# Gate and up of a two-layer decoder step: eight block products become seven on 14 of 22 tiles

## The chip, the cores and the metric

One of the NeuronCores of a Trainium2 chip runs the whole program in one launch. The metric is the device time of that program in microseconds (us); lower is better. Engines are named as in the profile: PE is TensorE (matmul) and PEld its weight load, DVE is VectorE, ACT is ScalarE, POOL is GpSimd, SP is the engine whose queue issues most transfers.

## The reference

One inference step of a two-layer decoder over 512 prompt tokens and 8 x 4 sample tokens, model width 1024, in fp32. Each layer is a macaron block:

```
x += 1/2 * SwiGLU(RMSNorm(x))                    # ffn1, width 2816
x += W_out [ tokmix(RMSNorm(x)) ; memxattn(...) ]
x += 1/2 * SwiGLU(RMSNorm(x))                    # ffn2, width 2816

def swiglu_half(x, g, w_gu, w_down):
    h = rmsnorm(x, g)
    gate, up = jnp.split(h @ w_gu, 2, axis=-1)
    return 0.5 * ((jax.nn.silu(gate) * up) @ w_down)
```

Layer 0 mixes tokens by gated linear attention, layer 1 by sliding-window attention with sinks over one shared key and value projection; both also attend to 256 memory tokens. A final RMSNorm follows. The caches, states and memory projections are outputs too. The four feed forwards hold most of the multiplications.

## The kernel before, in words

The residual stream stays in SBUF, transposed: eight tiles of 128 features for each of two token halves. Half 0 has 288 columns (256 prompt tokens and the 32 sample tokens), half 1 has 256. `NH` holds these widths, `KD` is 8.

Every fp32 product is made from three matmuls of the faster fp32r type: `split_into` (lines 291 to 299) has ACT copy a tile to its rounded high part, and DVE subtracts to get the low part; line 320 then runs high x high, high x low and low x high. `dense` (lines 310 to 323) does this for one weight tile of up to 128 outputs: for each half in its list it runs all eight contraction tiles, three matmuls each, into one PSUM bank. All its matmuls are recorded on line 321. `weight` (301 to 308) loads the raw tile through SP's queue into one of three tiles `wr`, and splits it into `wh` and `wl` (`WB` has their counts).

A feed forward (`ffn`, lines 405 to 439) has 22 tiles f of 128 gate and 128 up outputs, cut into three chunks by `CHUNKS`. For every f it runs gate, then up, applies the activation (ACT) and the multiplication (DVE), and splits the product; after a chunk's f's it runs the eight down tiles m and adds them to the residual. One f's gate, one f's up, or one m is a unit: the generator yields after each. Chunks 1 and 2 run over both halves, each weight serving both. Chunk 0 (9 f's) runs for each half by itself, so that its units can fill the waits of the other half's attention: `layer` (1090 to 1140) weaves attention steps with such units, by the counts in `FILL` (lead, pad, hold, last, more). After chunk 2's gathering the sums of squares, `rstd` (355 to 383) makes the reciprocal root mean square through small matmuls, and `normed` (393 to 402) scales the eight tiles and splits them: the inputs of what follows.

Within an engine, instructions run in the order that the tile framework's planner writes from its own estimate of the timeline; `high_priority(offset=...)` lets an instruction be placed as if it stood so many instructions earlier. `AHEAD` (6000) is used for splits of weights and reads of banks, `SOON` (6500) for a norm, `LEAD` for attention. Temporaries are `NU` slots of 288 columns, handed out in the order in which they were given back. Tiles tagged `v`, `ld` and `ml` serve attention: values, states and masks, and memory caches.

Of the kernel before, what the change touches and what calls it, by code (L numbers as in the profile page):

```python
# [32 lines left out]
FT = FF // P  # L33
CHUNKS = ((0, 9), (9, 15), (15, 22))
EARLY = 2 * CHUNKS[0][1] + KD
# [144 lines left out]
class Ring:  # L180
    """A few tiles that temporaries take in turn."""

# [22 lines left out]
class Banks:  # L205
    """PSUM banks that a stream takes in turn."""

# [23 lines left out]
class Build:  # L231
    NU, NV, NLD, NML = 102, 13, 8, 3
    WB = (3, 3, 3)
    MIX = 10
    FIRST, AHEAD, SOON, LEAD = 20000, 6000, 6500, 3000
    FILL = ((7, 1, 8, 2, 3), (8, 2, 6, 0, 6))

    def __init__(self, ctx, tc, d):
        self.tc, self.nc, self.d = tc, tc.nc, d
        self.cp = ctx.enter_context(tc.tile_pool(name="cp", bufs=1))  # L240
        self.wp = ctx.enter_context(tc.tile_pool(name="wp", bufs=2))
        self.up = ctx.enter_context(tc.tile_pool(name="up", bufs=1))
        self.pp = ctx.enter_context(tc.tile_pool(name="pp", bufs=1, space=PSUM))
        self.acc, self.seen = [[], [], []], [0, 0, 0]
        self.free = deque(range(self.NU))
        self.used, self.early = {}, {}
        banks = [self.pp.tile([P, 512], F32, tag=f"bank{i}", name=f"bank{i}") for i in range(8)]
        self.bd, self.bt, self.bm_ = Banks(banks[:3] + banks[5:]), Banks(banks[3:5]), Banks(banks[6:])
        self.sqs, self.xns, self.gas = Ring(self, 3), Ring(self, 2), Ring(self, 4)

# [33 lines left out]

# [1 line left out]
    def split(self, src, n):  # L286
# [14 lines left out]
    def weight(self, src, kc, m, name):  # L301
        nc = self.nc
        r = self.wp.tile([P, kc, m], F32, tag="wr", name=name + "r", bufs=self.WB[0])
        nc.sync.dma_start(r, src)
        h, l = (self.wp.tile([P, kc, m], F32R, tag="w" + e, name=name + e, bufs=b) for e, b in zip("hl", self.WB[1:]))
        with self.tc.high_priority(offset=self.AHEAD):
            self.split_into(h, l, r)
        return h, l

    def dense(self, src, parts, name, m=P, order=None):  # L310
# [18 lines left out]

# [1 line left out]
    def stats(self, x, h):  # L331
# [23 lines left out]
    def rstd(self, h, banks=None, keep=True):  # L355
        """1 / rms of every token, the same on all partitions, from the sums of squares over the blocks."""
        acc, self.acc[h], self.seen[h] = self.acc[h], [], 0
# [45 lines left out]

# [1 line left out]
    def ffn(self, tag, c, halves, xs, gathered=(), tanh=False):  # L405
# [3 lines left out]
        gs = {h: [] for h in halves}  # L409
        parts = [xs[h] for h in halves]  # L410
        for f in range(f0, f1):
# [28 lines left out]

# [1 line left out]
    def mem_load(self, k):  # L442
# [45 lines left out]

# [1 line left out]
    def mem_prompt(self, l, mq, mo):  # L490
# [115 lines left out]

# [1 line left out]
    def blocks(self, h):  # L608
# [254 lines left out]

# [1 line left out]
    def rope(self, ps, out, h, n=P):  # L865
# [51 lines left out]

# [1 line left out]
    def in_b(self, h, xs, s):  # L919
# [168 lines left out]

# [1 line left out]
    def layer(self, l, project, attend, w_out, xs):  # L1090
        """xs: the halves' inputs of the first feed forward; returns the inputs of what follows."""
        s = [Share(), Share()]
# [3 lines left out]
        def enter(h, norm):  # L1096
# [4 lines left out]
            return out  # L1101

        lead, pad, hold, last, more = self.FILL[l]
        drain(self.ffn(f1, 1, (0, 1), xs), self.ffn(f1, 2, (0, 1), xs, gathered=(0,)))
        self.drop(xs[0])
        late = self.ffn(f1, 0, (1,), xs, gathered=(1,), tanh=True)
# [24 lines left out]
        drain(self.out_proj(w_out, s[1].toks + s[1].mo, 1))  # L1131
        out[1] = enter(1, f"ffn2_{l}")
        drain(early)
        drain(self.ffn(f2, 1, (0, 1), out), self.ffn(f2, 2, (0, 1), out, gathered=(0,)))
        self.drop(out[0])

# [31 lines left out]
    def run(self):  # L1168
# [8 lines left out]
        self.vt, self.state, self.st = [None] * 5, [None] * GH, [None] * NB  # L1177
        self.x = [[], []]
        with self.tc.high_priority(offset=self.FIRST):
            self.gains = self.const("gains")  # L1180
# [26 lines left out]
        r = self.rstd(1)  # L1207
        xs[1] = self.normed(1, "ffn1_0", r)
        self.drop(r)
# [28 lines left out]
        drain(self.shared_kv(1, xk))  # L1238
        xs[1] = self.normed(1, "ffn1_1", r)
        self.drop(r)  # L1240
# [78 lines left out]
```

## Time and profile before

| | us |
|---|---|
| median of 3 runs | 2229.39 (2227.86 to 2230.09) |
| profiled execution, span from first to last instruction | 2228.3 |
| PE busy | 2192.8 (98%) |
| DVE busy | 1242.6 (56%) |
| ACT busy | 922.9 (41%) |
| mean granted TensorE clock | 0.990 |

The profiled execution's own time is its span and little around it: the span lies 1.1 us under the median of the runs. The profile lists the busy time of each engine, groups of instructions by line and tile, the waits and what ended them, and a timeline. A matmul's row gives its duration from start to the last result, about 0.28 to 0.30 us, while the next one starts after 0.12 to 0.13 us: the price of a matmul in a stream is the distance of starts, that is, a stretch of time over the number in it.

### The profile page before, as it was taken

How to read it: one execution, taken by the hardware profiler on the slowest of the kernel's cores; microseconds unless marked ns; L12 is line 12 of the kernel's file. 1: busy time of each engine (PE TensorE's matmuls, PEld its weight loads, DVE VectorE, ACT ScalarE, POOL GpSimd, SP SyncE). 2: the span in 40 equal slices, each digit the busy share in tenths (PEclk: the TensorE clock that was granted, in tenths of full speed). 3: DMA queues.
4: the chain of work that ended last, by engine and by line, in shares of the span. 5: the costliest groups of instructions: out<-in, count | busy, mean ns of one | idle time of the engine just before them, and what ended most of it. 6: DMA issues, size and time to landing. Idle time of an engine off the chain costs nothing.

```text
span 2228.3 us, 40781 instructions
## 1 busy us (share of the span) xinstructions
PE 2192.8 (98%) x16822; PEld 2106.3 (95%) x16822; DVE 1242.6 (56%) x2556; ACT 922.9 (41%) x1767; POOL 35.2 (2%) x69
## 2 busy tenths in 40 slices
PE   7999999999999999999999999999999999999998
PEld 6999999998699999999999999999888889999998
DVE  7633336586568865333577433337767766433355
ACT  4522224664556554222455322224534544322244
POOL 5000000000000000000000000000000000000000
PEclk8999999999999999999999999999989999999999
DMA  8532223444455344232364522224434334322244
GB/s 268 169 112 84 95 86 124 142 129 136 136 167 168 111 143 127 76 101 86 110 199 160 172 92 90 86 86 148 139 113 134 124 100 150 101 81 95 85 153 135
DMA packets 91546, 279.30 MB, mean 125 GB/s; under 512 B 11440, under 2 KB 25280, under 8 KB 91328
## 3 DMA queue, kind: packets, MB, share of 16 engines
q1 hardware_dynamic: 90784, 276.17, 39.4%
q8 instruction: 132, 2.16, 0.4%
q10 hardware_dynamic: 576, 0.52, 0.1%
q14 instruction: 54, 0.44, 0.1%
HBM read 270.33 MB, written 7.70 MB: 125 GB/s over the span
## 4 chain that ended last, share of the span: by engine, by line
PE 96%; ACT 1%; DVE 1%; issue 1%; DMA 1%; POOL 0%; SPq 0%; DVEq 0%; ACTq 0%
PE bank L321 85%; PE bank L960 1%; PE bank L735 1%; PE bank L575 1%; PE bank L502 1%; PE bank L855 1%; PE bank L974 1%; PE bank L523 1%; PE bank L973 1%; PE bank L847 1%; PE bank L549 0%; PE bank L365 0%; PE bank L377 0%; PE bank L514 0%; PE bank L995 0%
## 5 line engine op out<-in xcount | busy, mean ns | idle before, releaser
L294 ACT ACTIVATE u<-u 128x288 fp32r<-128x288 f32 (+2 forms) x308 | 124.3, 417 | 164.3 <-DVE u L425 130.6
L433 DVE SCALAR_TENSOR_TENSOR x<-bank,x 128x288 f32<-128x288 f32 (+1 forms) x192 | 84.6, 440 | 183.1 <-PE bank L321 182.8
L425 DVE TENSOR_TENSOR u<-u,bank 128x288 f32<-128x288 f32 (+1 forms) x176 | 76.7, 436 | 145.6 <-PE bank L321 144.4
L295 DVE TENSOR_TENSOR u<-u,u 128x288 fp32r<-128x288 f32 (+2 forms) x308 | 128.3, 430 | 33.5 <-ACT u L294 31.9
L420 ACT ACTIVATE u<-bank 128x288 f32<-128x288 f32 (+1 forms) x122 | 47.5, 390 | 98.7 <-PE bank L321 98.6
L321 PE MATMUL bank<-u,d0h 128*128 128x288 f32 (+1 forms) x352 | 70.3, 290 | 0.0
L321 PE MATMUL bank<-u,d1h 128*128 128x288 f32 (+1 forms) x352 | 68.9, 289 | 0.0
L321 PE MATMUL bank<-u,d2h 128*128 128x288 f32 (+1 forms) x352 | 68.3, 290 | 0.2 <-DVE x L598 0.2
L321 PE MATMUL bank<-u,d7h 128*128 128x288 f32 (+1 forms) x352 | 68.4, 291 | 0.0
L321 PE MATMUL bank<-u,d3h 128*128 128x288 f32 (+1 forms) x352 | 68.2, 290 | 0.0
L321 PE MATMUL bank<-u,d5h 128*128 128x288 f32 (+1 forms) x352 | 67.9, 290 | 0.1
L321 PE MATMUL bank<-u,d4h 128*128 128x288 f32 (+1 forms) x352 | 67.7, 289 | 0.0
L321 PE MATMUL bank<-u,d6h 128*128 128x288 f32 (+1 forms) x352 | 67.3, 288 | 0.0
L341 ACT ACTIVATE u<-x 128x288 f32<-128x288 f32 (+1 forms) x78 | 32.7, 422 | 64.9 <-DVE x L433 61.7
L321 PEld LDWEIGHTS bank<-u,d0h 128*128 128x128 f32 x352 | 56.2, 188 | 0.9 <-issue 0.8
L321 PEld LDWEIGHTS bank<-u,d7h 128*128 128x128 f32 x352 | 56.0, 190 | 0.8 <-issue 0.8
L321 PEld LDWEIGHTS bank<-u,d5h 128*128 128x128 f32 x352 | 55.3, 189 | 1.2 <-issue 1.2
L321 PEld LDWEIGHTS bank<-u,d4h 128*128 128x128 f32 x352 | 55.4, 188 | 0.7 <-issue 0.6
L321 PEld LDWEIGHTS bank<-u,d1h 128*128 128x128 f32 x352 | 55.7, 188 | 0.4 <-issue 0.4
L321 PEld LDWEIGHTS bank<-u,d2h 128*128 128x128 f32 x352 | 55.5, 189 | 0.3 <-issue 0.2
L321 PEld LDWEIGHTS bank<-u,d3h 128*128 128x128 f32 x352 | 55.6, 189 | 0.2 <-issue 0.2
L399 DVE SCALAR_TENSOR_TENSOR u<-x,gains,u 128x288 f32<-128x288 f32 (+1 forms) x112 | 53.2, 502 | 4.2 <-ACT u L382 4.0
(758 smaller groups left out, 7401.2 us busy)
## 6 DMA issues: line engine op xcount, KB each, us to landing
d0r<-dn_ffn SPq DMA_DIRECT2D x8, 576.0 KB, 3.9
d1r<-dn_ffn SPq DMA_DIRECT2D x8, 576.0 KB, 3.6
d2r<-dn_ffn SPq DMA_DIRECT2D x8, 576.0 KB, 3.9
d3r<-dn_ffn SPq DMA_DIRECT2D x8, 576.0 KB, 3.6
d4r<-dn_ffn SPq DMA_DIRECT2D x8, 576.0 KB, 3.8
d5r<-dn_ffn SPq DMA_DIRECT2D x8, 576.0 KB, 3.9
d6r<-dn_ffn SPq DMA_DIRECT2D x8, 576.0 KB, 3.7
d7r<-dn_ffn SPq DMA_DIRECT2D x8, 576.0 KB, 4.3
```

Source lines behind the costliest of these rows:

```text
L294: nc.scalar.activation(h, src, AF.Copy)
L295: nc.vector.tensor_tensor(out=l, in0=src, in1=h.bitcast(F32), op=ALU.subtract)
L321: self.nc.tensor.matmul(ps, w[:, k, :], x, start=i == 0 and j == 0, stop=i == kc - 1 and j == 2)
L341: nc.scalar.activation(sq, x, AF.Square)
L399: nc.vector.scalar_tensor_tensor(out=t, in0=self.x[h][k], scalar=self.gains[:, g, k:k + 1], in1=r, op0=ALU.mult, op1=ALU.mult)
L420: nc.scalar.activation(a, p, AF.Silu)
L425: nc.vector.tensor_tensor(out=a, in0=a, in1=p, op=ALU.mult)
L433: nc.vector.scalar_tensor_tensor(out=x, in0=po[i], scalar=0.25 if tanh else 0.5, in1=x, op0=ALU.mult, op1=ALU.add)
L502: nc.tensor.matmul(ps[:, b, :], mq[b][rows, tok], kt[b][rows], start=True, stop=True)
L523: nc.tensor.matmul(po[rows, (h // 2) * P:][:, :P], v[mt][:, 64 * h:64 * h + 64], pt[h][:, mt, :], start=mt == 0, stop=mt == 1)
L575: nc.tensor.matmul(po[:, :MT], pt[:, 4 * mt:4 * mt + 4].rearrange("p a t -> p (a t)"), vc[:, mt, :], start=b == 0 and mt == 0, stop=b == N ...
L735: nc.tensor.matmul(pv[:, c * half:(c + 1) * half], lhs[:, c * P:(c + 1) * P], second(rhs[:, c * P:(c + 1) * P]), start=True, stop=True)
```

## The change

The product of the two token halves with gate and up is a 2 x 2 block product: rows are the two halves of the contraction (four tiles each, `HK`), one factor's columns are gate and up, the other's are two token groups. Such a product takes eight block products as written, and seven by the scheme of Strassen and Winograd, at the price of sums of blocks ahead of and behind the products. The change does so for chunks 1 and 2 of every feed forward; `CHUNKS` now gives them 14 of 22 f's, and chunk 0 has 8.

- The token groups are two of 272 columns (`PW`): the first 272 of half 0, and half 1 with the last 16 columns of half 0.
- `pair` makes half 1's inputs (with the 16 columns added), splits them, and makes four forms, that is, sums and differences of input blocks, of four tiles each, also split. `form_tile` puts them in the tiles of attention that stand unused (`HOMES`) and in slots. `enter_pair` calls it after the output projection of half 1 ahead of ffn2; ahead of ffn1 it takes the place of `normed` for half 1.
- `quads` loads an f's gate and up tile together, makes four sums and differences of their halves on DVE, and splits gate, the two tiles of sums, and the second half of up.
- `ffn_pair` runs the seven products of an f, each four contraction tiles by three matmuls of 272 columns. One bank (`pb`) is seeded by ACT with a copy of the first product and then accumulated on. ACT and DVE read partial sums between products. The down tiles run over the two groups of 272, and three instead of two additions bring them to the residual.
- The slots are 97 instead of 102, raw weights keep 3 tiles, high and low parts get 4 each, sums of weights 2; the ring of activations has 6 instead of 4. `FILL` changes its counts.

```
-CHUNKS = ((0, 9), (9, 15), (15, 22))
+CHUNKS = ((0, 8), (8, 15), (15, 22))
+PW = (2 * P + NS + 2 * P) // 2
+HK = KD // 2
...
-    NU, NV, NLD, NML = 102, 13, 8, 3
-    WB = (3, 3, 3)
+    NU, NV, NLD, NML = 97, 13, 8, 3
+    WB = (3, 4, 4, 2)
     MIX = 10
     FIRST, AHEAD, SOON, LEAD = 20000, 6000, 6500, 3000
-    FILL = ((7, 1, 8, 2, 3), (8, 2, 6, 0, 6))
+    FILL = ((6, 1, 7, 2, 6), (7, 2, 5, 0, 9))
+    HOMES = ((13, 8, 3), (8, 8, 3))
 
     def __init__(self, ctx, tc, d):
         self.tc, self.nc, self.d = tc, tc.nc, d
...
         self.used, self.early = {}, {}
         banks = [self.pp.tile([P, 512], F32, tag=f"bank{i}", name=f"bank{i}") for i in range(8)]
         self.bd, self.bt, self.bm_ = Banks(banks[:3] + banks[5:]), Banks(banks[3:5]), Banks(banks[6:])
-        self.sqs, self.xns, self.gas = Ring(self, 3), Ring(self, 2), Ring(self, 4)
+        self.pb, self.pac = Banks(banks[3:5]), Banks(banks[5:])
+        self.sqs, self.xns, self.gas = Ring(self, 3), Ring(self, 2), Ring(self, 6)
 
...
-        h, l = (self.wp.tile([P, kc, m], F32R, tag="w" + e, name=name + e, bufs=b) for e, b in zip("hl", self.WB[1:]))
         with self.tc.high_priority(offset=self.AHEAD):
-            self.split_into(h, l, r)
+            return self.halved(r, name)
+    def halved(self, src, name):
+        h, l = (self.wp.tile(list(src.shape), F32R, tag="w" + e, name=name + e, bufs=b)
+                for e, b in zip("hl", self.WB[1:]))
+        self.split_into(h, l, src)
         return h, l
+    def quads(self, gu, f):
+        nc = self.nc
+        g, u = (self.wp.tile([P, KD, P], F32, tag="wr", name=f"{e}{f}r", bufs=self.WB[0]) for e in "gu")
+        nc.sync.dma_start(g, gu[f])
+        nc.sync.dma_start(u, gu[FT + f])
+        with self.tc.high_priority(offset=self.AHEAD):
+            gh, gl = self.halved(g, f"g{f}")
+            s, t = (self.wp.tile([P, KD, P], F32, tag="ws", name=f"{e}{f}s", bufs=self.WB[3]) for e in "st")
+            nc.vector.tensor_tensor(out=s[:, :HK], in0=u[:, :HK], in1=u[:, HK:], op=ALU.add)
+            nc.vector.tensor_tensor(out=s[:, HK:], in0=s[:, :HK], in1=g[:, :HK], op=ALU.subtract)
+            sh, sl = self.halved(s, f"s{f}")
+            nc.vector.tensor_tensor(out=t[:, :HK], in0=g[:, :HK], in1=u[:, :HK], op=ALU.subtract)
+            nc.vector.tensor_tensor(out=t[:, HK:], in0=g[:, HK:], in1=s[:, HK:], op=ALU.subtract)
+            th, tl = self.halved(t, f"t{f}")
+            uh, ul = self.halved(u[:, HK:], f"u{f}")
+        lo = lambda *w: tuple(a[:, :HK] for a in w)
+        hi = lambda *w: tuple(a[:, HK:] for a in w)
+        return lo(gh, gl), hi(gh, gl), lo(sh, sl), hi(sh, sl), lo(th, tl), hi(th, tl), (uh, ul)
+    def product(self, ps, w, xs, start):
+        wh, wl = w
+        for k, (xh, xl) in enumerate(xs):
+            for j, (a, x) in enumerate(((wh, xh), (wh, xl), (wl, xh))):
+                self.nc.tensor.matmul(ps, a[:, k, :], x, start=start and k == 0 and j == 0,
+                                      stop=k == len(xs) - 1 and j == 2, skip_group_check=True)
 
...
+    def pair(self, norm, r, xa):
+        nc = self.nc
+        g = NORMS.index(norm)
+        ts, cs = [self.u(PW) for _ in range(KD)], [self.u(PW) for _ in range(HK)]
+        xb = [None] * KD
+        forms, self.formed, self.extra = [], 0, []
+        for k in (0, 4, 1, 5, 2, 6, 3, 7):
+            nc.vector.scalar_tensor_tensor(out=ts[k][:, :NH[1]], in0=self.x[1][k], scalar=self.gains[:, g, k:k + 1],
+                                           in1=r, op0=ALU.mult, op1=ALU.mult)
+            nc.vector.tensor_tensor(out=ts[k][:, NH[1]:], in0=xa[k][0][:, PW:].bitcast(F32),
+                                    in1=xa[k][1][:, PW:].bitcast(F32), op=ALU.add)
+        part = lambda k, e: xa[k][e][:, :PW].bitcast(F32)
+        def form(srcs):
+            out = []
+            for s in srcs:
+                h, l = self.form_tile(), self.form_tile()
+                self.split_into(h, l, s)
+                out.append((h, l))
+            forms.append(out)
+        for k in range(HK):
+            nc.vector.tensor_tensor(out=cs[k], in0=ts[k], in1=part(k, 0), op=ALU.subtract)
+            nc.vector.tensor_tensor(out=cs[k], in0=cs[k], in1=part(k, 1), op=ALU.subtract)
+        form(cs)
+        for k in range(HK):
+            nc.vector.tensor_tensor(out=cs[k], in0=ts[k + HK], in1=cs[k], op=ALU.subtract)
+        form(cs)
+        for k in range(HK):
+            xb[k] = self.split(ts[k], PW)
+            nc.vector.tensor_tensor(out=ts[k], in0=ts[k + HK], in1=ts[k], op=ALU.subtract)
+        form(ts[:HK])
+        for k in range(HK):
+            xb[k + HK] = self.split(ts[k + HK], PW)
+            nc.vector.tensor_tensor(out=cs[k], in0=part(k + HK, 0), in1=cs[k], op=ALU.subtract)
+            nc.vector.tensor_tensor(out=cs[k], in0=cs[k], in1=part(k + HK, 1), op=ALU.add)
+        form(cs)
+        self.drop(ts, cs)
+        return xb, forms
+    def form_tile(self):
+        n, self.formed = self.formed, self.formed + 1
+        at = self.HOMES[self.layer_]
+        if n < at[0]:
+            return self.up.tile([P, PW], F32R, tag="v", name="fv", bufs=self.NV)
+        if n < at[0] + at[1]:
+            return self.up.tile([P, PW], F32R, tag="ld", name="fl", bufs=self.NLD)
+        if n < sum(at):
+            return self.up.tile([P, PW], F32R, tag="ml", name="fm", bufs=self.NML)
+        t = self.u(PW, F32R)
+        self.extra.append(t)
+        return t
+    def ffn_pair(self, tag, c, xs, gathered=()):
+        nc = self.nc
+        gu, dn = self.d["gu_" + tag], self.d["dn_" + tag]
+        f0, f1 = CHUNKS[c]
+        xa = [(h[:, :PW], l[:, :PW]) for h, l in xs[0]]
+        xb, (t1, t2, t3, t4) = xs[1], xs["forms"]
+        ga, gb = [], []
+        for bank in self.pb.banks:
+            nc.tensor.matmul(bank[:, :PW], xa[0][0][:, :P], xa[0][0], start=True, stop=True, skip_group_check=True)
+        for f in range(f0, f1):
+            w1, w2, s1, s2, s3, s4, w4 = self.quads(gu, f)
+            pa, pc, pb = (b()[:, :PW] for b in (self.pac, self.pac, self.pb))
+            c5, c2, act = (self.gas.u(PW) for _ in range(3))
+            ahead = lambda: self.tc.high_priority(offset=self.AHEAD)
+            self.product(pa, w1, xa[:HK], True)
+            with ahead():
+                nc.scalar.activation(pb, pa, AF.Copy)
+            self.product(pc, s1, t1, True)
+            self.product(pb, s2, t2, False)
+            with ahead():
+                nc.scalar.activation(c5, pc, AF.Copy)
+            self.product(pa, w2, xa[HK:], False)
+            with ahead():
+                nc.scalar.activation(c2, pb, AF.Copy)
+            self.product(pb, s3, t3, False)
+            with ahead():
+                nc.scalar.activation(act, pa, AF.Silu)
+                nc.vector.tensor_tensor(out=c5, in0=c5, in1=pb, op=ALU.add)
+            self.product(pc, s4, xb[HK:], False)
+            self.product(pb, w4, t4, False)
+            with ahead():
+                nc.vector.tensor_tensor(out=c2, in0=c2, in1=pc, op=ALU.add)
+                nc.scalar.activation(c2, c2, AF.Silu)
+                nc.vector.tensor_tensor(out=act, in0=act, in1=pb, op=ALU.mult)
+                ga.append(self.split(act, PW))
+                nc.vector.tensor_tensor(out=c2, in0=c2, in1=c5, op=ALU.mult)
+                gb.append(self.split(c2, PW))
+            yield
+        for m in range(KD):
+            po = self.dense(dn[m, :, f0:f1, :], [ga, gb], f"d{m}")
+            x0, x1 = self.x[0][m], self.x[1][m]
+            with self.tc.high_priority(offset=self.AHEAD):
+                for x, p in ((x0[:, :PW], po[0]), (x0[:, PW:], po[1][:, NH[1]:]), (x1, po[1][:, :NH[1]])):
+                    nc.vector.scalar_tensor_tensor(out=x, in0=p, scalar=0.5, in1=x, op0=ALU.mult, op1=ALU.add)
+            for h in gathered:
+                self.stats((x0, x1)[h], h)
+            if m == KD - 1:
+                self.drop(ga, gb)
+            yield
...
-        parts = [xs[h] for h in halves]
+        parts = [[(a[:, :NH[h]], b[:, :NH[h]]) for a, b in xs[h]] for h in halves]
...
+        def enter_pair(norm, xs):
+            with self.tc.high_priority(offset=self.SOON):
+                r = self.rstd(1)
+                xs[1], xs["forms"] = self.pair(norm, r, xs[0])
+            self.drop(r)
+        def both(tag, xs):
+            drain(self.ffn_pair(tag, 1, xs), self.ffn_pair(tag, 2, xs, gathered=(0,)))
+            self.drop(xs[0], self.extra)
         lead, pad, hold, last, more = self.FILL[l]
-        drain(self.ffn(f1, 1, (0, 1), xs), self.ffn(f1, 2, (0, 1), xs, gathered=(0,)))
-        self.drop(xs[0])
+        both(f1, xs)
         late = self.ffn(f1, 0, (1,), xs, gathered=(1,), tanh=True)
         mix[0] = enter(0, f"mix_{l}")
         drain(take(late, lead))
...
         drain(take(early, last))
         self.drop(s[1].q if l else [])
         drain(self.out_proj(w_out, s[1].toks + s[1].mo, 1))
-        out[1] = enter(1, f"ffn2_{l}")
+        enter_pair(f"ffn2_{l}", out)
         drain(early)
-        drain(self.ffn(f2, 1, (0, 1), out), self.ffn(f2, 2, (0, 1), out, gathered=(0,)))
-        self.drop(out[0])
+        both(f2, out)
 
...
+        self.layer_ = 0
...
-        xs[1] = self.normed(1, "ffn1_0", r)
+        xs[1], xs["forms"] = self.pair("ffn1_0", r, xs[0])
...
-        xs[1] = self.normed(1, "ffn1_1", r)
+        self.layer_ = 1
+        xs[1], xs["forms"] = self.pair("ffn1_1", r, xs[0])
```

Docstrings and comments that go are left out.

## The prediction

> **What bounds the kernel now.** I read the page's shares and its chain of waits first, then the windows by stage, then the groups by form, then the timeline where the change cuts in.
>
> ```profile
> span 2228.3 us, 40781 instructions
> ...
> PE 2192.8 (98%) x16822; PEld 2106.3 (95%) x16822; DVE 1242.6 (56%) x2556; ACT 922.9 (41%) x1767; POOL 35.2 (2%) x69
> ...
> PE 96%; ACT 1%; DVE 1%; issue 1%; DMA 1%; POOL 0%; SPq 0%; DVEq 0%; ACTq 0%
> ```
>
> TensorE is the bound: it has 35.5 us without work, and 96% of the chain is its own. Fewer matmuls shorten the run, unless another engine becomes the pace. So I need the price of a matmul and the room on DVE and ACT. Windows of line 321 alone (columns: stretch, length, PE busy and count, weight loads, clock, DMA):
>
> ```profile
> 100.00:120.00 20.00, 20.00 (x153) 20.00 (x152) 1.00 0.53 162
> 2160.00:2180.00 20.00, 19.91 (x167) 19.92 (x168) 1.00 0.74 233
> 124.00:172.00 48.00, 48.00 (x384) 48.00 (x383) 1.00 0.29 96
> ```
>
> The first stretch has only half 0 (288 columns): without the two at its edges 151 matmuls, 132 ns each. The second has only half 1 (256 columns): 119 to 120 ns; I take 119. The third is gate and up over both halves: 125 ns, so an f of 96 matmuls takes 12.0 us. The other engines in such a stretch, and in the attention of half 1 in layer 0 (PE, PEld, DVE, ACT, POOL):
>
> ```profile
> 144.00:192.00 48.00, 48.00 (x387) 48.00 (x386) 16.21 (x24) 14.00 (x24) 0.00 (x0) 1.00 0.27 79
> 686.00:818.00 132.00, 131.55 (x1021) 128.29 (x1021) 105.76 (x282) 81.12 (x191) 1.11 (x6) 1.00 0.42 136
> ```
>
> DVE has 4.05 us of work in 12.0 us per f: that is the room the change spends.
>
> **The change, part by part.** *Matmuls.* 13 ns for 32 columns puts 272 at 125.5 ns. Before, a feed forward has 22 x 96 = 2112 gate and up matmuls, half of each width: 1056 x 132 + 1056 x 119 = 265.1 us. After, 8 f's stay (384 x 132 + 384 x 119 = 96.4) and 14 take 7 x 4 x 3 = 84 matmuls of 272 (1176 x 125.5 = 147.6), together 244.0. The down products keep their number and mean width. Saved: 21.1 per feed forward, 84.3 us for four. 272 columns are in no row: at the price of 288 the gain, down products included, would be 36.6 us, at that of 256 it would be 132.6. I take the middle, since the width is the middle. Two dummy matmuls in each of the eight pair stages cost 16 x 0.125 = 2 us. [...]
>
> *DVE and ACT in a paired f.* Groups by form (columns: busy us, mean ns of one, idle before it; five of DVE, of which the fifth, from the windows of 192 to 234 us, splits a down weight, then three of ACT):
>
> ```profile
> L295 DVE TENSOR_TENSOR u<-u,u 128x288 fp32r<-128x288 f32 x150 | 66.7, 454 | 29.0 <-ACT u L294 28.2
> L295 DVE TENSOR_TENSOR u<-u,u 128x256 fp32r<-128x256 f32 x150 | 61.4, 418 | 3.2 <-ACT u L294 2.6
> L295 DVE TENSOR_TENSOR g4l<-g4r,g4h 128x1024 fp32r<-128x1024 f32 x8 | 9.8, 1224 | 1.8 <-ACT g4h L294 1.8
> L399 DVE SCALAR_TENSOR_TENSOR u<-x,gains,u 128x256 f32<-128x256 f32 x56 | 25.5, 479 | 3.2 <-ACT u L382 3.0
> L295 DVE TENSOR_TENSOR d1l<-d1r,d1h 128x768 fp32r<-128x768 f32 x1 | 1.0, 959 | 4.7 <-ACT d1h L294 4.7
> L294 ACT ACTIVATE g4h<-g4r 128x1024 fp32r<-128x1024 f32 x8 | 8.5, 1061 | 8.9 <-PE bank L321 6.7 <-issue 1.6 <-ACT u L987 0.6
> L420 ACT ACTIVATE u<-bank 128x256 f32<-128x256 f32 x52 | 19.1, 367 | 0.0
> L420 ACT ACTIVATE u<-bank 128x288 f32<-128x288 f32 x70 | 28.5, 408 | 98.7 <-PE bank L321 98.6
> ```
>
> On DVE, 512 columns lie midway between 256 and 768: 688 ns; 272 are 436. A paired f has three low parts of 1024 (3.67), four sums and one low part of 512 (3.44) and six operations of 272 (2.62): 9.73 us. ACT has three copies of 1024, one of 512 (about 0.63) and seven of 272 (0.39 to 0.42): 6.6 us. TensorE takes 84 x 125.5 = 10.54 us. In the timeline a low part and what follows it:
>
> ```profile
> 151.12 0.42 DVE L425 TENSOR_TENSOR u<-u,bank 128x256 f32<-128x256 f32 x1 [1.41 <-PE bank L321]
> 152.15 1.23 DVE L295 TENSOR_TENSOR g12l<-g12r,g12h 128x1024 fp32r<-128x1024 f32 x1 [0.60 <-ACT g12h L294]
> 153.29 0.42 DVE L295 TENSOR_TENSOR u<-u,u 128x256 fp32r<-128x256 f32 x1
> 163.12 0.42 DVE L425 TENSOR_TENSOR u<-u,bank 128x256 f32<-128x256 f32 x1 [1.41 <-PE bank L321]
> ```
>
> The next starts 0.09 us before the long one ends, so 14 operations back to back occupy 8.5 us. But each low part waits 0.60 us for its copy where nothing fills in. With 8.5 to 9.7 of 10.54 us, TensorE still paces the f, narrowly; the time would be gone if waits add 2 us.
>
> *Handovers.* Three reads of a bank now stand between products: the copy that seeds the second bank, the copy taken from it, and DVE's sum. Each has one product, 12 x 125.5 = 1.51 us, as cover.
>
> ```profile
> 153.96 0.30 PE L321 MATMUL bank<-u,g11l 128*128 128x288 f32 x1
> 154.35 0.41 ACT L420 ACTIVATE u<-bank 128x288 f32<-128x288 f32 x1 [1.94 <-PE bank L321]
> ...
> 49.08 0.41 ACT L420 ACTIVATE u<-bank 128x288 f32<-128x288 f32 x1
> 49.54 0.53 PE L321 MATMUL bank<-u,u1h 128*128 128x288 f32 x2 [0.29 <-ACT u L420]
> ```
>
> From the last matmul's start to the read 0.39 us, the read 0.39, to the next matmul 0.05: 0.83, of which 0.13 is the matmul's own slot. That leaves 0.8 us. A free engine loses nothing; one that has just begun a 1024 copy (1.06) or low part (1.22) is late by 0.26 or 0.4 us. Bounds per f: 0 to 0.9 us. The big copies come free when a product ends, behind the read that has the same moment and an earlier place, so I take 0.15: 56 x 0.15 = 8.4 us.
>
> *Weight transfers.* Bytes are the same; the ring of three raw tiles now gives up two per f.
>
> ```profile
> u1r<-gu_ffn SPq DMA_DIRECT2D x8, 512.0 KB, 3.7
> ```
>
> The up tile is asked for when the gate's low part of the f before is made, about 1 us before that f starts, and is needed some 6 us later: nothing. If the tile came free an f later, each f would wait up to 3.7 us. The forms also sit in the tiles of the mask, state and memory loads, so those leave SP's queue, and POOL's cast of the masks runs, only after the paired stage:
>
> ```profile
> L743 DVE COPY_PREDICATED u<-masks,bank x40: 266/294/450, 458.2 to 770.1; 128x128 f32<-128x128 uint8 x40
> L844 SPq DMA_DIRECT2D st<-state x16: 312/370/507, 41.1 to 579.2; - x16
> ```
>
> The masks' first reader starts at 458 us and the paired f's of layer 0's first feed forward end near 316 (from 124, 13 f's of 12.0 us and 288 down products of 125 ns): nothing. A load that the queue held ahead of weights would stop TensorE for as long as it waits.
>
> *Pair inputs.* pair() replaces half 1's eight scalings and eight splits (8 x 0.90 = 7.2 us of DVE) by eight scalings (3.8), eight adds of 16 columns (about 1.4 in all, taken as 0.17 each an estimate: 1.1 ns a column as between the rows of 256 and 288, and the same start-up), 24 sums and 24 low parts of 272 (21.0): 26 us, or 20.4 in steps 0.09 shorter. At the entry of ffn1 18 and 14 units of half 0 follow, a unit being 24 x 132 = 3.17 us: 57 and 44 us, which hide it. At ffn2 it starts only after the output projection and the norm:
>
> ```profile
> 846.36 0.40 PE L321 MATMUL bank<-u,op7h 128*128 128x256 f32 x2
> ...
> 858.42 0.88 DVE L399 SCALAR_TENSOR_TENSOR u<-x,gains,u 128x256 f32<-128x256 f32 x2 [0.60 <-ACT u L382]
> ...
> 1879.32 0.28 PE L321 MATMUL bank<-u,op7l 128*128 128x256 f32 x1
> ...
> 1891.14 0.88 DVE L399 SCALAR_TENSOR_TENSOR u<-x,gains,u 128x256 f32<-128x256 f32 x2 [0.36 <-ACT u L382]
> ```
>
> That is 11.8 us after the projection. FILL keeps 6 units there in layer 0 (3 before) and 9 in layer 1 (6 before): TensorE has 19.0 and 28.5 us. The first form is ready at about 20 us, when product 2 wants it at 20.5. The last is ready at 11.8 + 20.4 = 32, wanted by product 7 at 28 and 37.6. The weights' low parts and first reads of the same stretch, about 7.6 us of DVE, come between. Layer 0: 4 to 12 us, I take 10, since both queue on one engine; layer 1: 0 to 6, I take 2. What waits behind is the next f's weights.
>
> *Less fill.* The attention of half 1 gets 16 and 15 units in place of 21 and 20: 5 x 3.17 = 15.8 us less cover each. In layer 0's window above DVE works 105.8 of 132 us, and 116 would be left, so it still fits: 0 to 15.8 each, I take 3 together. The attention of half 0 keeps its number of units.
>
> **Sum:** 2228.3 - 84.3 + 2.0 + 8.4 + 12 + 3 = 2169.4. The median shown, 2229.39, is 1.1 above the profiled span, so 2170.
>
> **Rivals.** *DVE paces the f, mildly.* If 1.5 us of waits per f stay unfilled: 9.73 + 1.5 = 11.2 us, 0.7 above TensorE, 39 us in place of 8.4: 2201. For it: an f leaves DVE under 2 us; against: four f's of rows show DVE idle two thirds, and the split order can be moved.
> *DVE paces it past the old f (slower).* An f has six copy and low-part pairs; if none of their waits (0.55 each) is filled, 9.73 + 3.3 = 13.0 us, 2.5 above TensorE, 140 us: about 2300. It decides at 11.8 us per f, 2 us of unfilled waits. Against: DVE's queue has other ready work in every wait.
> *All hidden.* Handovers free, entries covered: 2228.3 - 82.3 = 2146, with the offset 2148.
> *The entry stall halves the clock.* Clock windows:
>
> ```profile
> 567.60:574.40 6.80, 6.54 (x20) 4.00 (x20) 4.41 (x18) 2.60 (x8) 0.00 (x0) 0.50 0.77 229
> 676.00:684.00 8.00, 5.54 (x48) 5.47 (x49) 5.18 (x10) 6.14 (x11) 0.31 (x1) 1.00 0.53 175
> ```
>
> A gap of 2.4 us left the clock at 1.00; a stretch of 20 matmuls in 6.8 us ran at 0.50. If the entry's stall comes in one piece, 6.8 us at half speed cost 3.4 at each ffn2: 2177. [...] Against it: the stall is spread over four products.
> *It doesn't cut time per matmul:* the bound at 288's price above, 2170 + 48 = 2218.
>
> **How the numbers follow.** Forecast 0.46 (its own range 2155 to 2187), all hidden 0.14, half clock 0.06, DVE mildly 0.18, no cheaper matmul 0.04, DVE past the old f 0.12. 2148 to 2222 leaves out the last and a part of the edges. Within 0.2% (4.5 us, what a measurement can tell) lies only a strip around 11.8 us per f: 0.03. Faster 0.85, slower 0.12.
>
> **What would show it.** Matmul windows at 125 to 126 ns in paired stretches, 84 to an f; successive f's of ffn_pair 10.6 to 10.8 us apart; PE waits on ACT and DVE there of 0.3 us or less, under 10 us in all; after the projection in layer 0 waits of TensorE for low parts of the forms adding to about 10 us. An f of over 11.2 us with DVE above nine tenths would prove the forecast wrong.

## The result, and the profile after

The changed kernel takes 2195.32 us (median of 4 runs, 2194.42 to 2206.89) against 2229.74 (4 runs) before: a ratio of 0.9847, interval 0.9819 to 0.9876. It gains 34 us where 59 were forecast: inside the range, 2148 to 2222, but outside the forecast's own, 2155 to 2187. The loss against the forecast, 25 us, is what the experiments look for. The profiled execution took 2195.54 us, 1.7 above its span.

The page of the changed kernel (span; busy time by engine; chain of waits):

```profile
span 2193.8 us, 40498 instructions
...
PE 2127.1 (97%) x16166; PEld 2035.5 (93%) x16166; DVE 1544.0 (70%) x3246; ACT 1067.2 (49%) x2101; POOL 36.3 (2%) x69
...
PE 83%; DVE 8%; DMA 4%; issue 2%; ACT 1%; SPq 0%; DVEq 0%; ACTq 0%
```

There are 656 matmuls fewer, the 672 less and the 16 dummies more of the sum. TensorE is idle for 66.7 us instead of 35.5, and DVE has come into the chain. The paired f's themselves, first the windows of the products' line alone, then one stretch with all engines (columns as before):

```profile
120.00:140.00 20.00, 20.00 (x162) 20.00 (x161) 1.00 0.34 106
140.00:160.00 20.00, 20.00 (x162) 20.00 (x161) 1.00 0.30 101
```

```profile
120.00:180.00 60.00, 60.00 (x481) 60.00 (x480) 48.48 (x78) 33.60 (x61) 0.00 (x0) 1.00 0.30 97
```

The groups of the tiles `fv`, which hold the early forms, give the first start of the same product in each f (duration min/median/max, first and last start over the kernel):

```profile
L342 PE MATMUL bank<-fv,s10h x42: 284/287/291, 138.7 to 1902.4; 128*128 128x272 f32 x42
...
L342 PE MATMUL bank<-fv,s14h x42: 284/287/296, 180.8 to 1944.6; 128*128 128x272 f32 x42
```

Four f's from 138.7 to 180.8 are 10.53 us each: 84 matmuls at 125.4 ns with nothing between them. DVE works 48.48 of 60 us, 8.5 in an f, the lower of the two values of the prediction. So in the paired stage the change does what the sum says. The loss lies outside; the waits of TensorE over the run (us in total, times, longest):

```profile
PE bank L356 <- DVE u L561: 8.1, 3, 2.7
...
PE bank L845 <- DVE o L838: 4.9, 1, 4.9
PE bank L356 <- ACT u L362: 2.8, 1, 2.8
...
PE bank L342 <- ACT s8h L298: 2.5, 1, 2.5
PE bank L342 <- DVE fv L299: 2.4, 1, 2.4
```

Four things are new here: three waits of 2.7 us for DVE's L561 (the last step of a tanh unit of chunk 0), one of 4.9 us for the output of layer 0's attention of half 1, one of 2.8 us for L362 (a copy out of a bank) in front of a unit at 1226 us, and the waits for the first sums and forms at the two entries of ffn2. Beside them the granted clock fell:

```profile
core 0: 2193.8 us, clock 0.981
```

It was 0.990. In both traces the granted clock is 1.00 or 0.50 at every time (0.59 over a window is a mixture), so at half rate lie 2193.8 x 0.019 x 2 = 83 us (45 before). A window behind the first of the three waits, and two in the entries of ffn2 (PE, its count, clock, DMA in the first pair; PE, PEld, DVE, ACT, POOL, clock, DMA in the second):

```profile
371.40:374.80 3.40, 3.40 (x19) 0.50 0.70 237
374.80:378.20 3.40, 3.40 (x28) 1.00 0.08 30
```

```profile
858.00:866.00 8.00, 6.22 (x26) 5.91 (x27) 8.00 (x19) 2.15 (x7) 0.00 (x0) 0.59 0.21 66
1878.00:1887.00 9.00, 7.01 (x32) 6.80 (x33) 9.00 (x18) 5.71 (x11) 0.00 (x0) 0.62 0.37 117
```

TensorE was busy all of the 3.4 us behind the wait, and made 19 matmuls; the next 3.4 us, at full rate, have 28, though most of these are wider. In the entries DVE has no free moment. The price of half rate is read from the kernel's own runs: spans of 2193.8 us at clock 0.981 and 2205.1 at 0.976 have 83 and 106 us at half rate, 22 more for 11 us more: half a microsecond for each. That is one pair: over the 53 runs of the changed kernel and of all experiments, each compared with the mean of its own kernel, it is 0.36 us. Where the text prices half rate, it gives both.

Where the three waits come from shows in the timeline at the end of layer 0's ffn1 (start, duration, engine, line). Before:

```profile
358.18 0.29 PE L321 MATMUL bank<-u,d7l 128*128 128x288 f32 x1
...
358.67 0.28 PE L365 MATMUL bank<-ones,u 128*128 128x1 f32 x2
...
361.03 0.94 PE L365 MATMUL bank<-ones,u 128*128 128x1 f32 x10
361.89 0.50 PE L321 MATMUL bank<-u,g0h 128*128 128x256 f32 x2
```

The last down product over half 0 ended at 358.5, and the norm's last sums of squares (L365, at 361.03) ran behind the product over half 1 and ahead of the first unit of the next stage. After:

```profile
350.19 0.29 PE L356 MATMUL bank<-u,d7l 128*128 128x272 f32 x1
350.32 0.28 PE L400 MATMUL bank<-ones,u 128*128 128x1 f32 x2
...
354.08 0.94 PE L400 MATMUL bank<-ones,u 128*128 128x1 f32 x10
...
360.70 0.94 PE L412 MATMUL bank<-u,ones 128*128 128x128 f32 x6
...
367.23 0.28 PE L356 MATMUL bank<-u,g1l 128*128 128x256 f32 x1
...
370.69 0.50 PE L356 MATMUL bank<-u,u2h 128*128 128x256 f32 x2 [2.70 <-DVE u L561]
```

```profile
367.43 1.06 ACT L298 ACTIVATE a_kh<-a_kr 128x1024 fp32r<-128x1024 f32 x1 [0.76 <-PE bank L356]
368.51 1.28 ACT L560 ACT_TABLE_LOAD   x1
369.80 0.38 ACT L560 ACTIVATE u<-bank 128x256 f32<-128x256 f32 x1
```

Now 16 columns of half 0 come out of the second group's product, so the last statistic waits for the very last down product, and its sums (L400, at 354.08) run only behind the first unit of the next stage. The norm takes two of the ring of three banks, first for its sums (L400), then for its broadcast (L412). The order of the chunk's units becomes g0, u0, u1, g2, g1, u2: g1 has been put behind the broadcast's bank, and u2, the next on TensorE, needs the bank that g1's tanh still reads. g1's last matmul starts at 367.23; its tanh starts at 369.80, behind a weight's copy of 1.06 us and a table load of 1.28, and DVE's step on it follows at 370.22.

### The profile page after: what moved, and what is told of

It reads as the page before. It is cut to its first block, busy times and chain, and to the rows that moved or that the text cites. A ratio compares the mean times of both kernels' runs of the same rounds, so it can differ in the third digit from the quotient of the medians.

```text
span 2193.8 us, 40498 instructions
## 1 busy us (share of the span) xinstructions
PE 2127.1 (97%) x16166; PEld 2035.5 (93%) x16166; DVE 1544.0 (70%) x3246; ACT 1067.2 (49%) x2101; POOL 36.3 (2%) x69
## 4 chain that ended last, share of the span: by engine, by line
PE 83%; DVE 8%; DMA 4%; issue 2%; ACT 1%; SPq 0%; DVEq 0%; ACTq 0%
PE bank L356 54%; PE bank L342 18%; PE bank L878 1%; PE bank L1103 1%; DMA u19r<-gu_ffn 1%; DMA u20r<-gu_ffn 1%; DMA u21r<-gu_ffn 1%; DMA u18r<-gu_ffn 1%; PE bank L645 1%; PE bank L998 1%; PE bank L990 1%; PE bank L1117 1%; PE bank L1116 1%; DVE u L299 1%; PE bank L666 1%
## 5 line engine op out<-in xcount | busy, mean ns | idle before, releaser
L298 ACT ACTIVATE u<-u 128x272 fp32r<-128x272 f32 (+3 forms) x328 | 133.3, 421 | 121.7 <-DVE u L533 47.6
L299 DVE TENSOR_TENSOR u<-u,u 128x272 fp32r<-128x272 f32 (+3 forms) x328 | 137.3, 429 | 8.2 <-ACT u L298 7.1
L356 PE MATMUL bank<-u,d0h 128*128 128x272 f32 (+2 forms) x352 | 71.6, 290 | 0.0
L356 PE MATMUL bank<-u,d1h 128*128 128x272 f32 (+2 forms) x352 | 70.8, 288 | 0.0
L356 PE MATMUL bank<-u,d2h 128*128 128x272 f32 (+2 forms) x352 | 68.4, 289 | 0.4 <-DVE x L741 0.4
L356 PE MATMUL bank<-u,d3h 128*128 128x272 f32 (+2 forms) x352 | 68.3, 290 | 0.0
L356 PE MATMUL bank<-u,d4h 128*128 128x272 f32 (+2 forms) x352 | 67.3, 288 | 0.0
L356 PE MATMUL bank<-u,d5h 128*128 128x272 f32 (+2 forms) x352 | 67.1, 288 | 0.0
L356 PE MATMUL bank<-u,d7h 128*128 128x272 f32 (+2 forms) x352 | 67.0, 288 | 0.0
L356 PE MATMUL bank<-u,d6h 128*128 128x272 f32 (+2 forms) x352 | 66.8, 288 | 0.0
```

What stands on the lines that cost most here:

```text
L298: nc.scalar.activation(h, src, AF.Copy)
L299: nc.vector.tensor_tensor(out=l, in0=src, in1=h.bitcast(F32), op=ALU.subtract)
L356: self.nc.tensor.matmul(ps, w[:, k, :], x, start=i == 0 and j == 0, stop=i == kc - 1 and j == 2)
```

## The experiments

The expectations name their theories by letters. S: the loss is in the seams (entries of ffn2, norms, attention's fill), D: DVE paces the paired f's. Later, for the three waits, B: the norm's use of the three-bank ring, N: the late start of the norm.

**Is a product really worth its matmuls, and does DVE pace them?** An eighth product, and in a second kernel the two sums of up and gate made three times:

```diff
             self.product(pb, w4, t4, False)
+            self.product(pa, w4, t4, False)
```
```diff
-            nc.vector.tensor_tensor(out=s[:, :HK], ...)
-            nc.vector.tensor_tensor(out=s[:, HK:], ...)
+            for _ in range(3):
+                nc.vector.tensor_tensor(out=s[:, :HK], ...)
+                nc.vector.tensor_tensor(out=s[:, HK:], ...)
```

> An eighth product is put back into every paired f: the last one is run once more into a bank that is read no more, so the outputs stay the same. It adds 56 x 12 = 672 matmuls of 272 columns and no work for DVE or ACT. The changed kernel took 2195. Theory S (seams: the paired f's run at TensorE's pace, and the 25 us missing from the forecast were lost where stages meet, in waits at the norms and the attention's end and in stretches of half clock): every added matmul shows, 672 x 125.5 ns = 84 us, so 2279 (2273 to 2285). Theory D (DVE paces the paired f's, which lose 25 us / 56 = 0.45 us each): the longer f gives DVE its time back, so the f grows by 1.5 - 0.45 us only: +59, 2254.

> DVE makes the first two of the four weight sums of every paired f three times over (same values): 4 more operations of 512 columns, 0.60 us each back to back, 2.4 us an f. Theory S: DVE goes from 8.5 to 9.7 us up to 10.9 to 12.1 of TensorE's 10.54, so it just becomes the pace: +0.4 to +1.6 us an f, +22 to +90, 2217 to 2285. Theory D: DVE is the pace already and every added operation shows: 2.4 to 2.8 us an f, +135 to +155, 2330 to 2350.

The eighth product: 2288.49 us, ratio to before 1.0262 (1.0246 to 1.0277), 93 us over the changed kernel. Its 672 matmuls are 84.3 us at 125.5 ns; clock 0.977 gives 22 us more at half rate, worth 8 to 11 us, which S had left out (it gave at most 2285). D falls: under D the added work of TensorE would have hidden beside DVE. The sums three times: 2248.32 us, ratio 1.0077 (1.0048 to 1.0105), 53 us more. Windows of all engines in its paired f's:

```profile
130.00:180.00 50.00, 48.34 (x372) 46.79 (x372) 48.12 (x79) 27.14 (x51) 0.00 (x0) 1.00 0.29 89
```

DVE got 135 us of work more (1679.3 us in the page against 1544.0), 2.4 us an f, and is now as busy as TensorE. 82 of the 135 us did not show, 1.5 us an f: the margin between 8.5 and 10.53 us is real, and not much more than this. In this kernel the entries wait longest, 9.2 us in one piece in layer 1.

**The entries of ffn2.** The forms left out, and half 1's plain splits in their place in the products:

```diff
-        form(cs)
...
+        forms = [xb[:HK], xb[HK:], xb[:HK], xb[HK:]]
```

> pair() makes no forms: the 24 sums and the 16 low and high parts of the forms are left out, and the four products that read forms read half 1's own split tiles instead; the outputs of the feed forwards are other numbers. All matmuls stay. Theory S: TensorE's waits behind pair() at the two ffn2 entries go (5.0 us in layer 0, 4.5 in layer 1), and so do the stretches of half clock that begin there (6.8 us at half rate each, 3.4 us lost each): -16 us, 2179; the other seams stay. Theory D: DVE has 14 us less in each pair() but no less in the 56 f's: 2190 to 2195.

2180.01 us, ratio 0.9776 (0.9761 to 0.9791): 15 us less than the changed kernel, and the waits for `fv`, s8h and s8l are gone; the three of 2.7 us stay. The wait of 2.8 us at 1226 us is gone too, with one of 1.2 in its place, so the 15 us are not the two entries alone.

**More units around the norms.** Two units moved from behind the output projection of half 0 to ahead of its input projection:

```diff
-    FILL = ((6, 1, 7, 2, 6), (7, 2, 5, 0, 9))
+    FILL = ((8, 1, 5, 2, 6), (9, 2, 3, 0, 9))
```

> FILL's lead is two units longer (8 and 9 for 6 and 7) and its hold two shorter (5 and 3 for 7 and 5), so that the attentions keep their number of units. In the changed kernel TensorE waits 2.7 us at 371 and at 1525 us for a bank whose tanh stands in ACT's queue behind the split of a projection weight; with the longer lead the tanh stands ahead of it. Theory S: both waits go, and the half clock after them (3.4 us at half rate each): -5.4 - 3.4 = -9 us, 2186. Rival H: two units less stand behind the output projection of half 0, so a wait of the same size opens at that norm: 2195 or up to 2200.

2204.91 us, ratio 0.9888 (0.987 to 0.9905), 10 us worse; both expectations missed. The waits for L561 are still there, longest 2.7 us. That they came from too few units ahead of the projection's splits is refuted. New waits of 1.1 to 2.1 us, three of them between 698 and 710 us, fit that the units are missed where they were taken; it was not tested. What was left to test for the three waits was the order inside the chunk: ring or late norm. One kernel gives the norms of half 0 the pair of banks that the products used until then; one leaves out the 16 columns' addition in the last down tile.

```diff
-        mix[0] = enter(0, f"mix_{l}")
+        mix[0] = enter(0, f"mix_{l}", self.pac)
...
-        r = self.rstd(0)
+        r = self.rstd(0, self.pac)
```
```diff
                 for x, p in (...):
+                    if gathered and m == KD - 1 and p is not po[0] and x is not x1:
+                        continue
```

> The norms of half 0 that follow a paired feed forward (mix in both layers, kv between them) take their two PSUM banks from banks 5 to 7, which the paired f's have just left, and not from the ring of three that the units take. Same numbers, same matmuls. In the changed kernel TensorE waits 2.7 us behind each of these norms, at 371, 1113 and 1525 us: unit g1 has the bank that the norm's broadcast sits in, so it runs last and u2 waits for its tanh. Theory B (the ring of banks alone makes the wait): the three waits go with the half clock behind them (3.4 + 6.8 + 3.4 us, half of it lost): -8.1 - 6.8 = -15 us against 2195, so 2180. Theory N (the norm itself starts late: half 0's last statistic now needs both down products of the last tile, 21 matmuls or 2.6 us more): the wait moves to the projection that reads the norm, and 0 to -5 us are won: 2190 to 2195.

> In the last down tile of the second paired chunk the 16 columns of half 0 that sit in token group b are not added to the residual (left out; the outputs are other numbers there). Half 0's last statistic then needs the first down product alone, as before the change. Theory N (late start of the norm): its start moves 2.6 us earlier at 351, 1093 and 1505 us, TensorE's waits of 2.7 us go and the half clock behind them: -15 us against 2195, 2180. Theory B (ring of banks): the unit that shares the bank still waits for the norm, though a norm 2.6 us earlier: -3 us, 2192.

Other banks: 2177.42 us, ratio 0.9768 (0.9743 to 0.9793). No 16 columns: 2179.74, ratio 0.977 (0.9753 to 0.9788). Each takes 16 to 18 us off, and in each no wait for L561 is left. With the other banks the units run g0, u0, g1, u1, g2, u2. So N and B are not rivals: the wait needs both, the late norm and the shared ring, and goes with either. In the profiled runs the other banks take TensorE's gaps of over 0.3 us from 58.5 to 47.4 us, 8.1 of it the three waits, and half rate from 83 to 70 us, worth 5 to 7: together about the 17 us by which the spans differ.

**The regrouping by itself.** `CHUNKS` and `FILL` of the changed kernel in the kernel before, no paired product:

```diff
-CHUNKS = ((0, 9), (9, 15), (15, 22))
+CHUNKS = ((0, 8), (8, 15), (15, 22))
-    FILL = ((7, 1, 8, 2, 3), (8, 2, 6, 0, 6))
+    FILL = ((6, 1, 7, 2, 6), (7, 2, 5, 0, 9))
```

> The kernel before with the changed CHUNKS and FILL alone: eight products, no pair inputs, chunk 0 of 8 f's. It tells what the regrouping of units costs without the seven products. Theory S: the attention of half 1 in layer 0 lacks the five units and ends with the same wait of about 5 us and 3.4 us lost to half clock: 2229 + 8 = 2237; its norms show no 2.7 us waits. Rival: the waits of the changed kernel come from the tiles that its forms hold and from DVE's load: 2229 within 3.

2241.27 us, ratio 1.0043 (1.0028 to 1.0058), 10.5 us slower than before. Its new wait, at the end of layer 0's attention of half 1:

```profile
PE bank L321 <- DVE u L295: 2.2, 1, 2.2
```

The matmuls are the same, so 10.5 us is the price of the regrouping, more than either expectation gave. This one wait is 2.2 us of it; TensorE's gaps of over 0.3 us add to 37.6 us against 27.5, spread over short waits between 550 and 860 us and between 1680 and 1880 us. That the five units less make them is not shown. From here the seven products bring 46 us.

**More units at the entries.** Three more kept for them:

```diff
-    FILL = ((6, 1, 7, 2, 6), (7, 2, 5, 0, 9))
+    FILL = ((6, 1, 7, 2, 9), (7, 2, 5, 0, 12))
```

> FILL keeps three more units for ffn2's entry, 9 and 12 for 6 and 9, which the attentions of half 1 lose. Theory S: the entries' waits (5.0 and 4.5 us) and the half clock behind them (6.8 us each, half of it lost) go, -16; the wait at the end of layer 0's attention (4.9 us at 800 us) grows by up to three units of 3.17 us, +5 to +10: together 2184 to 2190. Rival: the attentions still have enough, 2179.

2200.47 us, ratio 0.9863 (0.9846 to 0.9879), 5 us worse; both expectations missed. The entry of layer 1 now has one wait of 5.6 us for L561 in front of a down product, at the end of the kept units:

```profile
PE bank L356 <- DVE u L561: 13.7, 4, 5.6
```

Units of chunk 0 need DVE too; more of them do not cover what DVE has to do there. The wait at the end of layer 0's attention did not grow with three more units taken from it: it is 4.0 us in place of 4.9. In the kernel with the longer lead, which has as many units under that attention as the changed kernel, no wait there is over 0.9 us. So the number of units does not set that wait; what does stays open.

**Do the two losses add, and can the entry be shortened?** Four kernels: the other banks and no forms together; the other banks with the adds of 16 columns on GpSimd; the other banks with the four splits that the products don't read made last; the other banks once more.

```diff
-            nc.vector.tensor_tensor(out=ts[k][:, NH[1]:], ...)
+            nc.gpsimd.tensor_tensor(out=ts[k][:, NH[1]:], ...)
```
```diff
-            xb[k] = self.split(ts[k], PW)
-            nc.vector.tensor_tensor(out=ts[k], in0=ts[k + HK], in1=ts[k], op=ALU.subtract)
+            nc.vector.tensor_tensor(out=es[k], in0=ts[k + HK], in1=ts[k], op=ALU.subtract)
...
+        for k in range(HK):
+            xb[k] = self.split(ts[k], PW)
```

> The changed kernel with both edits at once: the norms of half 0 that close a feed forward take their banks from the pair that the products use (alone 18 us under the changed kernel), and the forms of the inputs are not made, the products reading half 1's plain splits in their place, so that the output is not the feed forward's (alone 15 us under). Theory: the wait behind the late norm and the wait for the forms are two separate losses. Then the gains add: about 2162 us, no wait of TensorE of 2.7 us at the three norms, no wait of over 1 us in the two entries of ffn2, and 60 to 70 us of half clock. Rival: both edits only spare the same stretches of half clock, so that the second adds little: 2172 to 2178. If the time falls under 2170 the loss against the forecast is these two items and nothing else.

> The other banks for the norms of half 0, and the eight adds of 16 columns of each entry on GpSimd in place of VectorE. Theory: at the entry of ffn2 VectorE is the pace, so 8 adds of about 0.17 us less bring the last form 1.4 us forward there: 2173 to 2177, waits at the two entries about 7 us in place of 9.5. Rival: GpSimd's adds start late or hold VectorE up, and the forms come no earlier or later: 2177 to 2183.

> The other banks for the norms of half 0, and in each entry the four splits of half 1's first four tiles, which no product of the paired stage reads, are made after the last form in place of ahead of the third one. Theory: VectorE is the pace of the entry, so 4 low parts of 0.36 us less ahead of the third and fourth form bring these 1.4 us forward: 2174 to 2177. Rival: the waits of the entry are for the first form's low parts and for the weights' low parts, not for the third and fourth form: then nothing moves, 2177 to 2179.

> The kernel with the other banks alone once more, beside the three above on the same chip: 2177 us, 0.977 of the kernel before, within 0.2% of its first timing.

Together 2161.05 us, ratio 0.9684 (0.9668 to 0.9699): 2195.3 - 17.9 - 15.3 = 2162.1 was to be expected from the two alone. They are two separate losses. The entries of ffn2 in the changed kernel (PE, its count, clock, DMA):

```profile
836.00:876.00 40.00, 34.90 (x240) 0.91 0.21 66
1846.00:1890.00 44.00, 39.39 (x275) 0.92 0.27 87
```

and with the forms alone left out, in stretches of the same length and place behind the output projection:

```profile
831.20:871.20 40.00, 39.86 (x311) 1.00 0.29 93
1839.50:1883.50 44.00, 44.00 (x343) 1.00 0.35 109
```

139 matmuls more in the two stretches, 17 us at 125 ns; of it 9.6 are idle time, and 7 the clock (0.09 x 40 and 0.08 x 44).

The other banks again: 2178.41, ratio 0.9764 (0.9747 to 0.978), as the first time; it is the fastest version here that leaves nothing out. The adds on GpSimd: 2184.91, ratio 0.9796 (0.978 to 0.9812), 6.5 us worse; splits last: 2188.19, ratio 0.9798 (0.9779 to 0.9817), 9.8 worse. Both are slower than either of their expectations, though their intervals touch that of the other banks alone. TensorE's longest waits in the entries are no shorter with the first:

```profile
PE bank L342 <- ACT s8h L298: 2.5, 1, 2.5
PE bank L342 <- DVE fv L299: 2.4, 1, 2.4
```

With the second the same two places wait 2.6 us, for a form's copy on ACT, and 1.9, in front of a down product. So neither the eight small adds nor the four splits alone set those waits. TensorE's gaps of over 0.3 us add to 48 or 49 us in these two kernels and in the one with the banks alone. What differs is the time at half rate, 74 and 83 us against 65, worth 3 to 4 and 6 to 9 us; the profiled spans are 4.9 and 9.1 us apart. Why it grew by so much is not settled.

## Why the prediction was right or wrong

- **Matmuls, -84.3.** Right: 125.4 ns at 272 columns, 10.53 us an f, and the eighth product gives the price back. The rival without a cheaper matmul falls with it.
- **DVE in the paired f.** Right: 8.5 us of 10.53. Both rivals in which DVE paces it are refuted by the windows; the threefold sums show that some 1.5 us of room was all there was.
- **Handovers, +8.4.** Mis-sized: outside the entries the products waited under 1 us in the whole run (10.0 us of waits of line 342 are in the list, of which 9.5 in the entries). The reads of a bank do come in time, as the 0.8 us of margin said; the 0.15 us for a late engine was not paid.
- **Weight transfers, masks, first feed forward's entries: nothing.** Right; no wait of the products for a DMA is in the list of waits. The room is small, though: the page's chain now passes through the transfers of the up tiles u18 to u21 (DMA has 4% of it against 1% before).
- **Entries of ffn2, +12 (10 and 2).** The place is right, layers and form are not: waits of 5.0 us in layer 0 and 4.5 in layer 1, at the earliest forms and the sums of the first f's weights, not at the last form. The step that failed is the one that has the first form ready about 20 us behind the projection. The eight scalings begin 11.9 us behind it in layer 0, as forecast (11.8), and 13.4 in layer 1, but the first low part of the first form begins 29.6 and 29.3 us behind it; the projection's last matmul starts at 829.57 us in layer 0:

```profile
841.51 3.25 DVE L448 SCALAR_TENSOR_TENSOR u<-x,gains,u 128x256 f32<-128x256 f32 x8
...
859.17 0.78 DVE L299 TENSOR_TENSOR fv<-u,fv 128x272 fp32r<-128x272 f32 x2
```

In the order that the scheduler made, DVE does the weights' sums and low parts, half 1's plain splits and the later forms' sums in between, and it is busy all the time in the windows of both layers. Leaving the forms out gains 15 us, 16 to 17 with the other banks, half rate and the wait at 1226 us included.

- **Less fill, +3.** Mis-sized: regrouping alone cost 10.5 us. "It still fits" was argued from DVE's sum over 132 us of window, 116 of 132. Such a sum does not show which result ends last: the long wait is for one of DVE's results at the end of the attention. Why the regrouping costs so much stays open.
- **Missing from the sum: the norms of half 0, 18 us.** The prediction put the 16 columns on the side of DVE's adds, and did not follow who waits for the last of them: the statistic of half 0, the norm, and behind it the ring of banks.
- **Half rate.** A rival with 0.06, tied to the entries. It is real and wider: 38 us more at half rate, some 14 to 19 us of time, behind the norms and at the attention's end too. It is counted in the sums above.
- **A slip of arithmetic.** "All hidden" adds up to 2147, not 2148; the forecast does not rest on it.

With the measured sizes (the dummies' 2.0 as forecast): 2228.3 - 84.3 + 2.0 + 1 + 15.3 + 10.5 + 18 = 2190.8, and 1.7 around the span give 2192.5. Of the last 3 us, 1.4 lie in the first 60 us, where TensorE's waits add to 16.4 us against 15.0; the rest was not looked into.

That the total came inside the range is in part luck. An oversized term took the place of an omitted one, and the range reached up to 2195 only for rivals that did not happen: DVE as the pace, at 2201, and matmuls at the price of 288 columns, at 2218.

## What to carry to other kernels

Fewer products by sums of blocks pay what the matmuls cost as long as the other engines' work per product stays under TensorE's; here that held with 1.5 to 2 us an f to spare (DVE 8.5 of 10.53 us), and 2.4 us more for DVE cost 53 us over 56 f's. The price is at the seams: when a group of columns is cut anew, follow the last column of each half to the norm or statistic that waits for it, and give small side work banks of its own. Count cover by what ends last at the end of a stage, not by an engine's share over it, and look for half rate behind each wait of TensorE of over 2 us: here 38 of the 47 of 2.2 to 2.8 us had it, and all 14 of 4.0 us and more.

## What was not expected of the hardware

The granted clock fell to half behind waits shorter than the stretch that follows: in the changed kernel 3.4 us at 0.50 from 371.4 us, behind a wait of 2.70. In the profiles of all kernels here, from the first feed forward on, 47 waits of TensorE lasted 2.2 to 2.8 us, and 38 of them had a stretch at half rate that began in the wait or within 3.5 us behind it; all 14 of 4.0 us and more had one. In the traces before and after, those that end within the run last 3.4, 6.8, 10.2, 13.7 or 17.1 us, one to five times 3.4. Not every one follows a wait: the longest in the changed kernel, 17.1 us from 545.4, lies among small matmuls of the attention, with no wait of over 0.6 us ahead of it. The same program twice, the same wait of 2.77 us (timelines; first timing and second timing of the kernel with the other banks):

```profile
1212.46 0.71 PE L356 MATMUL bank<-u,g5h 128*128 128x288 f32 x2 [2.77 <-ACT u L362]
```

```profile
1212.91 0.53 PE L356 MATMUL bank<-u,g5h 128*128 128x288 f32 x2 [2.77 <-ACT u L362]
```

In the first the rate was halved behind it (0.71 us for two matmuls, granted clock 0.58 from 1212 to 1216 us), in the second it was not (0.53 us, 1.00). Nor does the length of the wait tell the two apart: in the changed kernel one of 2.41 us, up to 859.65, came with 6.8 us at 0.50 from 859.5 on; one of 2.44 us in the kernel before (675.65 to 678.09), the gap that the prediction cites as leaving the clock at 1.00, was one of the nine exceptions. What decides it is not shown by these runs.
